# The indexer's query-key products with both parts of a query head stacked in the array's 128 rows

## The chip, the cores and the metric

One core of a Trainium2 chip runs the program in one launch. The metric is the device time of that launch in microseconds. Below, PE is TensorE, DVE is VectorE, ACT is ScalarE, POOL is GpSimd and SP is SyncE, which issues most of the transfers.

## What is computed

One layer of a decoder block on 512 tokens of width 1024, all in fp32:

```
h = rms_norm(x);  proj = h @ w_in            # columns for all mixers and gates
# A: sparse attention; the indexer picks 128 causal keys for each query
dots  = einsum('bqhd,bsd->bqhs', iq, ik)     # 8 index heads of 64, one key head
score = einsum('bqh,bqhs->bqs', iw, relu(dots))
sel   = top_k(causal(score), 128)
y_att = softmax attention of 8 heads over the selected keys
# B: chunked gated DeltaNet, 4 heads of 128, after a short convolution
# merge
x = x + (sigmoid(ga) * (y_att @ w_att) + sigmoid(gb) * (y_dn @ w_dn)) @ w_o
# PEER: 8 product-key heads, top 16 each, over 128 * 128 experts
x = x + peer(rms_norm(x))
```

## The kernel before, in words

Activations lie transposed: features on the 128 partitions, the 512 tokens along the free axis. Most products are made in a split format: an fp32 operand is written as a high part of type fp32r, which ACT copies, and a low part, which DVE gets by subtraction (`split`), and three fp32r products stand for one fp32 product (`mm3`).

**First stage (to about 464 us of the profile).** `project(ct)` makes 128 of the projection's columns: it loads a weight tile `wt` of 512 KB, splits it into `wh` and `wl`, and does 24 products. The tiles `wt`, `wh` and `wl` come from the pool `pp`, two buffers each. 43 such projections follow each other: one small one with the index keys, 12 convolved ones for the DeltaNet, 4 index queries (`CT_IQ`), 4 for the output gate z, k, v, 4 attention queries, and 16 merge gates, which are stored to DRAM (`sgd`). From the sixth on they are the filler of four chains that run step by step in turn: two DeltaNet pairs, the indexer and the attention. After each step of a chain, a fraction `FILL_A` or `FILL_B` of a projection's step is added, and `tc.issue_after` ties it to a product of that chain. A scheduler then sets the order on each engine from its own estimate of times.

**The indexer.** `projections()` copies the four results of 128 rows (two heads each) to `iqT`; the index keys are copied to rows 0 to 63 of `ikT`, and a transfer repeats them in rows 64 to 127. `index(tb)`, for blocks 1 to 3 of 128 queries, makes for each of the 8 heads one plain fp32 product of 64 rows:

```
            b = (h % 2) * 64
            dt = bank("at")
            mm(dt[:, :N], iqT[b:b + 64, h // 2, dsl], ikT[b:b + 64, :N])
```

N is 256, 384 or 512 keys. ACT takes the positive part, DVE adds it with its weight, and 16 rounds on DVE pick the top 128.

**Branches and output (464 to 561 us).** `attention_branch` makes 8 tiles (dt) of the attention branch: a gate is loaded back from `sgd` and passed through a sigmoid, half a weight tile of 256 KB goes through `wt`, `wh` and `wl`, 12 products follow. The DeltaNet branch does the same 8 times (L701 to L710 for the gate, the reading of the products and the sum, then a split of the sum into `mh` and `ml`). The output product takes 8 weight tiles of 512 KB, four for each half `cg` of the columns; block b of four has its bank `acc[b]`. In the second half, the weights of kp 0 and 1 go to tiles of their own (`late`), and block 3 is tied behind the transposes of block 0, which follow `second_norm(0)`. All of these weights pass through `wt` in `pp`, and so do the first two of the PEER query (`wq`).

**PEER (561 us to the end).** Its weights come from other pools (`wp`, `up`, `ex`): 128 tiles of u, a top-k, 128 tiles of v, and gathered rows for the last block of tokens.

Of the kernel before, what the change touches and what calls it, by code (L numbers as in the profile page):

```python
# [9 lines left out]
F32 = mybir.dt.float32  # L10
F32R = mybir.dt.float32r
# [4 lines left out]
ALU = mybir.AluOpType  # L16
# [3 lines left out]
P = 128  # L20
T = 512
D = 1024
NB = T // P
# [5 lines left out]
CT_DN, CT_SM, CT_IQ, CT_K, CT_V, CT_Q, CT_Z, CT_G = 0, 12, 13, 17, 18, 19, 23, 27  # L29
# [53 lines left out]
def tile_block(ctx, tc, x, xT, w_in, sc_cols, sc_rows, w_br, w_o, w_q, subT, uT, uv, cst, iota, out, dbg=None):  # L83
    nc = tc.nc
    dbg = dbg or {}
    V, S, G, PE = nc.vector, nc.scalar, nc.gpsimd, nc.tensor
# [3 lines left out]
    def mm(o, l, r, start=True, stop=True):  # L90
        hop[0] = PE.matmul(o, l, r, start=start, stop=stop).ins  # L91
# [9 lines left out]
    def load(dst, src):  # L101
        nc.sync.dma_start(dst, src)
# [5 lines left out]
    def pool(stack, name, **kw):  # L108
        return stack.enter_context(tc.tile_pool(name=name, bufs=1, **kw))
# [13 lines left out]
    hl = hp.tile([P, 8, T], F32R, name="hl", tag="hl")  # L123
    fm = pool(f1, "fm")
    pp = pool(px, "pp", side="right")
# [5 lines left out]
    def bank(tag, bufs=2):  # L131
        return ps.tile([P, T], F32, name=tag, tag=tag, bufs=bufs)

    def tmp(n=T, bufs=5):
        return pp.tile([P, n], F32, name="tmp", tag=f"tmp{n}", bufs=bufs)
# [30 lines left out]
    def split(hi, lo, src):  # L166
        S.copy(hi, src)  # L167
        return V.tensor_tensor(lo, src, hi.bitcast(F32), op=ALU.subtract).ins  # L168
# [16 lines left out]
    rb = bank("dn0")  # L185
    for tb in range(NB):
        mm(hs(rb, tb), r1[:, tb:tb + 1].to_broadcast([P, P]), ident)
    rbs = pp.tile([P, T], F32, name="rbs")
    S.copy(rbs, rb)
    lows = []  # L190
    for k in range(8):
# [3 lines left out]
        lows.append(split(hh[:, k, :], hl[:, k, :], xk))  # L195

    def weights(wp, src, shape=(8, P), dst=None):
        wt = wp.tile([P, *shape], F32, name="wt", bufs=2)
        load(wt, src)
        wh, wl = dst or (wp.tile([P, *shape], F32R, name=n, bufs=2) for n in ("wh", "wl"))  # L200
        split(wh, wl, wt)
        return wh, wl

    def project(ct):

        wh, wl = weights(pp, w_in[ct])
        o = bank("mm")
        for k in range(8):
            mm3(o, (wh[:, k, :], wl[:, k, :]), (hh[:, k, :], hl[:, k, :]), k == 0, k == 7)
            if k < 7:  # L210
                yield
        return o

    ikT = fm.tile([P, T], F32, name="ikT")
    iqT = fm.tile([P, 4, T], F32, name="iqT")
    kT = fm.tile([P, T], F32, name="kT")
    vtok = fm.tile([P, NB, P], F32, name="vtok")
    small = fm.tile([P, NB, 16], F32, name="small")
# [23 lines left out]
    both, early, o = project(CT_SM), conv(0), None  # L242
    while o is None:
        try:
            next(both)
        except StopIteration as e:
            o = e.value
        next(early)
    sm_ = tmp()
    S.copy(sm_, o)  # L250
    S.copy(ikT[0:64, :], o[0:64, :])
    nc.sync.dma_start(ikT[64:128, :], ikT[0:64, :])
    st = bank("at")
    for tb in range(NB):
        PE.transpose(st[:, tb * P:(tb + 1) * P], sm_[:, tb * P:(tb + 1) * P], ident)
    V.tensor_copy(small, st.rearrange("p (b c) -> p b c", c=P)[:, :, 64:80])
    t3 = [P, NB, 4]
    u = pp.tile(t3, F32, name="u")
    e = pp.tile(t3, F32, name="e")
    al = pp.tile([P, 4], F32, name="al")  # L260
    V.tensor_tensor(u, small[:, :, 8:12], dtb[:, None, :].to_broadcast(t3), op=ALU.add)
    V.scalar_tensor_tensor(e, u, -1.0, u, op0=ALU.mult, op1=ALU.min)
# [190 lines left out]

    def projections():
        for t in range(4):
            S.copy(iqT[:, t, :], (yield from project(CT_IQ + t)))
            if t == 3:
                done.add("index")
            yield
        for t in range(4):  # L460
            S.activation(szT[:, t, :], (yield from project(CT_Z + t)), AF.Silu)
            if t == 3:
                done.add("z")
            yield
        o = yield from project(CT_K)
        kk = tmp()
        S.activation(kk, o, AF.Square)
        kss = bank("at")
        mm(kss, blk64, kk)
        S.activation(kT, o, AF.Copy, scale=kg)  # L470
        V.tensor_scalar(kk, kss, 1.0 / 64, EPS, op0=ALU.mult, op1=ALU.add)
        rk = tmp()
        rsqrt(rk, kk, "k")
        V.tensor_tensor(kT, kT, rk, op=ALU.mult)
        yield
        o = yield from project(CT_V)
        va = tmp()
        S.copy(va, o)
        vt = bank("at")
        for tb in range(NB):  # L480
            PE.transpose(hs(vt, tb), hs(va, tb), ident)
        S.copy(vtok.rearrange("p b c -> p (b c)"), vt)
        yield
        for j in range(4):
            o = yield from project(CT_Q + j)
            S.activation(qT[:, j, :], o, AF.Copy, scale=qg)
            q2 = tmp()
            S.activation(q2, o, AF.Square)
            qs = bank("at")
            for tb in range(NB):  # L490
                mm(qs[:, tb * 2:tb * 2 + 2], hs(q2, tb), ind2)
            V.tensor_scalar(qsc[:, :, 2 * j:2 * j + 2], qs[:, :8].rearrange("p (b c) -> p b c", c=2), 1.0 / 64, EPS, op0=ALU.mult, op1=ALU.add)
            if j < 3:
                yield
        q_ = pp.tile([P, NB * 8], F32, name="q_")
        fl = qsc.rearrange("p b h -> p (b h)")
        rsqrt(q_, fl, "q")
        V.tensor_scalar(fl, q_, 0.125, None, op0=ALU.mult)
        done.add("attention")
        yield  # L500
        for t in (8 * br + dt for dt in range(8) for br in range(2)):
            o = yield from project(CT_G + t)
            s_ = tmp()
            S.copy(s_, o)
            nc.sync.dma_start(sgd[t], s_)
            yield
# [6 lines left out]
    def index(tb):  # L513
        N = (tb + 1) * P
        dsl = slice(tb * P, (tb + 1) * P)
        acc = row("acc", 1)
        for h in range(8):
            b = (h % 2) * 64
            dt = bank("at")
            mm(dt[:, :N], iqT[b:b + 64, h // 2, dsl], ikT[b:b + 64, :N])  # L520
            yield
            R = row("R", 2)
            S.activation(R[:, :N], dt[:, :N], AF.Relu)
            w = small[:, tb, h:h + 1]
            if h == 0:
                V.tensor_scalar(acc[:, :N], R[:, :N], w, 0.0, op0=ALU.mult, op1=ALU.add)
            else:
                V.scalar_tensor_tensor(acc[:, :N], R[:, :N], w, acc[:, :N], op0=ALU.mult, op1=ALU.add)
        V.tensor_tensor(acc[:, dsl], acc[:, dsl], cs("causneg"), op=ALU.add)
        wk = row("wk", 1)  # L530
        for r in range(16):
            m8 = aw.tile([P, 8], F32, name="m8", bufs=2)
            src = acc if r == 0 else wk
            V.max(m8, src[:, :N])
            V.match_replace(wk[:, :N], m8, src[:, :N], TAKEN)
        bias = row(f"bias{tb}", 1)
        V.scalar_tensor_tensor(bias[:, :N], wk[:, :N], 0.0, acc[:, :N], op0=ALU.add, op1=ALU.is_equal)
        V.tensor_scalar(bias[:, :N], bias[:, :N], -1e30, None, op0=ALU.mult)
        return bias
# [75 lines left out]
    def attention_branch():  # L615

        ya = hp.tile([P, 2, 4, T], F32R, name="ya", tag="hh")
        mixed = branch[0] = hp.tile([P, 8, T], F32, name="mixed", tag="hl")
        for k in range(4):
            split(ya[:, 0, k], ya[:, 1, k], qT[:, k, :])  # L620
        for dt in range(8):
            s_ = tmp()
            load(s_, sgd[dt])
            S.activation(s_, s_, AF.Sigmoid)
            wt = pp.tile([P, 8, P], F32, name="wt", bufs=2)[:, :4]
            load(wt, w_br[dt][:, :4])
            w = [pp.tile([P, 8, P], F32R, name=n, bufs=2)[:, :4] for n in ("wh", "wl")]
            split(*w, wt)
            o = bank("mm")
            for k in range(4):  # L630
                mm3(o, at(w, k), (ya[:, 0, k], ya[:, 1, k]), k == 0, k == 3)
                if k < 3:
                    yield
            V.tensor_tensor(mixed[:, dt, :], s_, o, op=ALU.mult)
            yield
# [62 lines left out]
    for dt in range(8):  # L698
        s_ = tmp()
        load(s_, sgd[8 + dt])  # L700
        S.activation(s_, s_, AF.Sigmoid)  # L701
        wt = pp.tile([P, 8, P], F32, name="wt", bufs=2)[:, :4]
        load(wt, w_br[dt][:, 4:])
        w = [pp.tile([P, 8, P], F32R, name=n, bufs=2)[:, :4] for n in ("wh", "wl")]
        split(*w, wt)
        o = bank("mm")
        for k in range(4):
            mm3(o, at(w, k), at(yd, k), k == 0, k == 3)
        V.tensor_tensor(s_, s_, o, op=ALU.mult)
        V.tensor_tensor(s_, s_, branch[0][:, dt, :], op=ALU.add)  # L710
        split(mt[0][:, dt, :], mt[1][:, dt, :], s_)
# [83 lines left out]
    wp = pool(wx, "wp", side="right", reuse_waits="tile")  # L795
# [41 lines left out]
    for h in range(8):  # L837
# [3 lines left out]
        for p in range(2):  # L841
            if h == 0:
                _, o = first_q[p]
            else:
                o = bank("mm")
# [159 lines left out]
    n, slot = 0, 0  # L1005
# [135 lines left out]
```

## Time and profile before

| | |
|---|---|
| median of 3 runs | 1843.3 us (1842.14 to 1844.12) |
| profiled execution, its own time | 1844.26 us |
| its span, first to last instruction | 1842.5 us |
| PE busy | 1791.8 us, 97% |
| DVE busy | 1442.0 us, 78% |
| ACT busy | 803.1 us, 44% |
| POOL busy | 188.6 us, 10% |
| mean granted clock of PE | 0.998 of full speed |

Times in the trace count from the span's start. A row of the timeline gives start, duration, engine, line and operation, the tile written and the tiles read, and in brackets how long the engine was idle before it and what ended that. Products on PE are pipelined: the distance of two starts is what one costs, and a row's own duration is longer. A plain fp32 product appears as two passes.

### The profile page before, as it was taken

What the parts mean: (1) busy time and instruction counts of PE and PEld (TensorE: products, weight loads), DVE (VectorE), ACT (ScalarE), POOL (GpSimd) and SP (SyncE); (2) the same over time, 40 slices, a digit from 0 to 9 for tenths busy, and PEclk for the clock granted to TensorE, in tenths of its full rate; (3) what the DMA queues carried; (4) which work ended last, traced back from release to release, by engine and by line L of the source; (5) the groups of instructions that cost most, each with busy time, mean ns of one, the idle gap of its engine ahead of it and who ended that gap; (6) DMA issues with size and microseconds to landing.
All of it is one profiled execution on the core that took longest, in us unless ns stands there. A gap on an engine that the chain in (4) does not pass through costs nothing.

```text
span 1842.5 us, 26292 instructions
## 1 busy us (share of the span) xinstructions
PE 1791.8 (97%) x9527; PEld 1572.5 (85%) x9527; DVE 1442.0 (78%) x3291; ACT 803.1 (44%) x1401; POOL 188.6 (10%) x132
## 2 busy tenths in 40 slices
PE   5999999999999999999999999999999999999998
PEld 4787677878788899999999988888888888888887
DVE  5767988654667899999997686788787887787886
ACT  5433434443533334555655444344443444343442
POOL 0000000000000000010000112122121222212220
PEclk9999999999999999999999999999999999999999
DMA  4211111111643214567676898989988988898974
GB/s 148 92 64 63 58 41 58 52 52 41 211 147 130 89 52 142 186 226 258 250 268 228 307 365 305 336 316 361 337 313 327 347 315 309 335 357 313 343 299 170
DMA packets 142354, 396.74 MB, mean 215 GB/s; under 512 B 10704, under 2 KB 71760, under 8 KB 122768
## 3 DMA queue, kind: packets, MB, share of 16 engines
q1 hardware_dynamic: 123792, 260.84, 40.3%
q0 software_dynamic: 18432, 134.23, 18.9%
q8 instruction: 75, 1.23, 0.3%
q14 instruction: 55, 0.45, 0.1%
HBM read 353.60 MB, written 41.29 MB: 214 GB/s over the span
## 4 chain that ended last, share of the span: by engine, by line
PE 82%; DVE 8%; DMA 6%; ACT 2%; issue 1%; SPq 0%; DVEq 0%; ACTq 0%
PE mm L91 28%; PE acc L91 25%; PE wo L91 6%; PE dn L91 5%; PE at L91 3%; DMA vt<-in_uv_dram 2%; DMA gt<-gd 2%; DVE ul L168 1%; DVE ob L986 1%; PE tr L91 1%; PE at L571 0%; PE dn L320 0%; DMA wt<-in_w_br_dram 0%; DVE tmp L229 0%; DVE gt L1046 0%
## 5 line engine op out<-in xcount | busy, mean ns | idle before, releaser
L91 PE MATMUL acc<-vl,ch 128*128 128x512 f32 x768 | 299.5, 390 | 1.1 <-DVE vl L1045 1.1
L91 PE MATMUL acc<-vh,cl 128*128 128x512 f32 x768 | 298.2, 389 | 0.0
L91 PE MATMUL acc<-vh,ch 128*128 128x512 f32 x768 | 263.1, 390 | 4.9 <-ACT vh L1044 4.9
L951 POOL DMA_INDIRECT row<-in_uv_dram,eidx x124 | 178.6, 1441 | 832.3 <-DVE x1g L963 775.1
L167 ACT CAST uh<-ut 128x1024 fp32r<-128x1024 f32 x128 | 134.6, 1051 | 150.0 <-PE mm L91 84.0
L1045 DVE TENSOR_TENSOR vl<-vt,vh 128x1024 fp32r<-128x1024 f32 x128 | 156.4, 1222 | 50.3 <-ACT vh L1044 47.6
L168 DVE TENSOR_TENSOR ul<-ut,uh 128x1024 fp32r<-128x1024 f32 x128 | 155.9, 1219 | 34.4 <-ACT uh L167 33.8
L91 PE MATMUL mm<-hTh,uh 128*128 128x384 f32 x496 | 168.6, 340 | 2.9 <-ACT gs L818 1.9
L91 PEld LDWEIGHTS acc<-vh,ch 128*128 128x128 f32 x768 | 143.3, 188 | 32.1 <-ACT vh L1044 6.6
L91 PE MATMUL mm<-hTh,ul 128*128 128x384 f32 x496 | 168.0, 340 | 2.7 <-DVE ul L168 2.7
L91 PEld LDWEIGHTS acc<-vl,ch 128*128 128x128 f32 x768 | 144.2, 188 | 30.2 <-DVE vl L1045 2.1
L963 DVE SCALAR_TENSOR_TENSOR x1g<-row,co,x1g 128x1024 f32<-128x1024 f32 x128 | 163.8, 1280 | 7.4 <-ACT co L962 5.3
L91 PEld LDWEIGHTS acc<-vh,cl 128*128 128x128 f32 x768 | 144.1, 188 | 29.2
L1044 ACT CAST vh<-vt 128x1024 fp32r<-128x1024 f32 x128 | 133.9, 1046 | 78.4 <-DMA vt<-in_uv_dram 64.0
L91 PE MATMUL mm<-hTl,uh 128*128 128x384 f32 x496 | 167.3, 337 | 0.0
L167 ACT CAST ch<-gt 128x384 fp32r<-128x384 f32 x128 | 65.5, 512 | 218.1 <-PE acc L91 211.1
L960 DVE CUSTOM_DVE_ANT_0 scr<-row,h2g 128x1024 f32<-128x1024 f32 x128 | 156.0, 1218 | 0.3
L91 PE MATMUL mm<-hh,wh 128*128 128x512 f32 x344 | 144.6, 424 | 3.6 <-ACT hh L167 2.1
L168 DVE TENSOR_TENSOR wl<-wt,wh 128x1024 fp32r<-128x1024 f32 (+1 forms) x81 | 90.1, 1115 | 63.4 <-ACT wh L167 63.2
L91 PE MATMUL mm<-hh,wl 128*128 128x512 f32 x344 | 137.3, 401 | 0.0
L91 PE MATMUL mm<-hl,wh 128*128 128x512 f32 x344 | 136.9, 398 | 0.0
L167 ACT CAST wh<-wt 128x1024 fp32r<-128x1024 f32 (+1 forms) x81 | 77.7, 962 | 110.9 <-PE mm L91 86.7
(818 smaller groups left out, 3765.8 us busy)
## 6 DMA issues: line engine op xcount, KB each, us to landing
ut<-in_uT_dram SPq DMA_DIRECT2D x128, 512.0 KB
vt<-in_uv_dram SPq DMA_DIRECT2D x128, 512.0 KB
gd<-gb SPq DMA_DIRECT2D x24, 1024.0 KB
gt<-gd SPq DMA_DIRECT2D x16, 1536.0 KB
wt<-in_w_in_dram SPq DMA_DIRECT2D x43, 512.0 KB
gs<-gs SPq DMA_DIRECT2D x84, 192.0 KB
wt<-in_w_q_dram SPq DMA_DIRECT2D x16, 512.0 KB
sgd<-tmp SPq DMA_DIRECT2D x16, 256.0 KB
```

The costliest lines, as they stand in the source:

```text
L91: hop[0] = PE.matmul(o, l, r, start=start, stop=stop).ins
L167: S.copy(hi, src)
L168: return V.tensor_tensor(lo, src, hi.bitcast(F32), op=ALU.subtract).ins
L951: G.indirect_dma_start(out=row.rearrange("p t d -> p (t d)"), out_offset=None, in_=uv, in_offset=bass.IndirectOffsetOnAxis(ap=released.get ...
L960: V.tensor_tensor_reduce(scr, row[:, 0], h2g, 1.0, 0.0, op0=ALU.mult, op1=ALU.add, accum_out=a)
L963: V.scalar_tensor_tensor(x1g, row[:, 1], co, x1g, op0=ALU.mult, op1=ALU.add)
L986: V.tensor_scalar(ob[:, t], io, sl[:, 1, n:n + 1], sl[:, 2, n:n + 1], op0=ALU.is_equal, op1=ALU.mult)
L1044: S.copy(vh, vt)
L1045: paced = V.tensor_tensor(vl, vt, vh.bitcast(F32), op=ALU.subtract)
```

## The change

The index operands are kept in split form, and a head's product takes all 128 rows. For each head, `iqS[:, h]` holds the high part in its own half of the rows and the low part in the other half. `ikS` holds the keys' high part in both halves, and in a second tile their low part in both halves. Two fp32r products of 128 rows, accumulated in one bank, then give all four partial products.

```
-    ikT = fm.tile([P, T], F32, name="ikT")
-    iqT = fm.tile([P, 4, T], F32, name="iqT")
+    ikS = [fm.tile([P, T], F32R, name=f"ik{n}") for n in "hl"]
+    iqS = fm.tile([P, 8, T], F32R, name="iqS")
...
-    S.copy(ikT[0:64, :], o[0:64, :])
-    nc.sync.dma_start(ikT[64:128, :], ikT[0:64, :])
+    S.copy(ikS[0][0:64, :], o[0:64, :])
+    V.tensor_tensor(ikS[1][0:64, :], o[0:64, :], ikS[0][0:64, :].bitcast(F32), op=ALU.subtract)
+    for part in ikS:
+        load(part[64:128, :].bitcast(F32), part[0:64, :].bitcast(F32))
...
-            S.copy(iqT[:, t, :], (yield from project(CT_IQ + t)))
+            o = yield from project(CT_IQ + t)
+            hi, lo = tmp().bitcast(F32R), tmp().bitcast(F32R)
+            split(hi, lo, o)
+            for i in range(2):
+                mine, other = slice(i * 64, i * 64 + 64), slice(64 - i * 64, 128 - i * 64)
+                load(iqS[mine, 2 * t + i, :].bitcast(F32), hi[mine].bitcast(F32))
+                load(iqS[other, 2 * t + i, :].bitcast(F32), lo[mine].bitcast(F32))
...
-            b = (h % 2) * 64
             dt = bank("at")
-            mm(dt[:, :N], iqT[b:b + 64, h // 2, dsl], ikT[b:b + 64, :N])
+            for i, part in enumerate(ikS):
+                mm(dt[:, :N], iqS[:, h, dsl], part[:, :N], i == 0, i == 1)
```

The larger tiles need room. The change takes it from `wt` in `pp`, which now has one buffer, in `weights` and in both branches, and from four small tiles (`rbs`, `u`, `e`, `q_`), which now come from the rotating `tmp`:

```
-        wt = wp.tile([P, *shape], F32, name="wt", bufs=2)
+        wt = wp.tile([P, *shape], F32, name="wt", bufs=1 if wp is pp else 2)
...
-            wt = pp.tile([P, 8, P], F32, name="wt", bufs=2)[:, :4]
+            wt = pp.tile([P, 8, P], F32, name="wt", bufs=1)[:, :4]
```

The order moves in three places that matter here. On SP, where the last gates are stored (`sgd`) and the first branch weights are loaded from `in_w_br_dram`, before:

```order
L505 DMA sgd6_296<-tmp_3799 128x512
L102 DMA wt_4192<-in_w_br_dram 128x512
L505 DMA sgd14_304<-tmp_3929 128x512
L102 DMA wt_4215<-in_w_br_dram 128x512
L505 DMA sgd7_297<-tmp_4065 128x512
L102 DMA tmp_4189<-sgd0_290 128x512
L102 DMA tmp_4212<-sgd1_291 128x512
L505 DMA sgd15_305<-tmp_4176 128x512
```

and now:

```order
L514 DMA sgd15_308<-tmp_4231 128x512
L102 DMA tmp_4267<-sgd1_294 128x512
L102 DMA wt_4270<-in_w_br_dram 128x512
L102 DMA tmp_4290<-sgd2_295 128x512
L102 DMA tmp_4313<-sgd3_296 128x512
L102 DMA tmp_4336<-sgd4_297 128x512
L102 DMA x1g_4441<-in_x_dram 128x1024
L102 DMA wt_4293<-in_w_br_dram 128x512
```

The second branch weight (`wt_4215`, now `wt_4270`) moved from ahead of the last two gate stores to behind them.

On DVE in the DeltaNet branch (the reading of the products at L709, now L718; the sum at L710, now L719; the weight's low part `wl` and the sum's low part `ml` at L168), before:

```order
L168 TENSOR_TENSOR wl_4522<-wt_4519,wh_4521 128x512
L709 TENSOR_TENSOR tmp_4490<-tmp_4490,mm_4499 128x512
L168 TENSOR_TENSOR ml_4411<-tmp_4464,mh_4410 128x512
L168 TENSOR_TENSOR wl_4548<-wt_4545,wh_4547 128x512
L710 TENSOR_TENSOR tmp_4490<-tmp_4490,mixed_4180 128x512
```

and now:

```order
L718 TENSOR_TENSOR tmp_4493<-tmp_4493,mm_4502 128x512
L168 TENSOR_TENSOR wl_4525<-wt_4522,wh_4524 128x512
L719 TENSOR_TENSOR tmp_4493<-tmp_4493,mixed_4235 128x512
L168 TENSOR_TENSOR ml_4466<-tmp_4493,mh_4465 128x512
L718 TENSOR_TENSOR tmp_4519<-tmp_4519,mm_4528 128x512
L168 TENSOR_TENSOR wl_4551<-wt_4548,wh_4550 128x512
```

Before, `wl_4522` is the weight of the step after `mm_4499` and stands ahead of the reading of `mm_4499`; now `wl_4525`, the weight of the step after `mm_4502`, stands behind the reading of `mm_4502`.

On PE at the end of the output product's second half (`wo_4748` to `wo_4751` are blocks 0 to 3, now `wo_4803` to `wo_4806`; `tr` are the transposes of block 0's norm `h2t`), before:

```order
L91 MATMUL wo_4750<-wh_4770,mh_4410 128x512
L91 MATMUL wo_4750<-wl_4771,mh_4410 128x512
L91 MATMUL wo_4750<-wh_4770,ml_4411 128x512
L728 MATMUL tr_4844<-C_92,h2t_4827 128x128 x4
L728 MATMUL tr_4851<-C_92,h2t_4827 128x128 x4
L91 MATMUL wo_4751<-wh_4752,mh_4410 128x512
```

and now:

```order
L91 MATMUL wo_4803<-wh_4825,ml_4466 128x512
L91 MATMUL wo_4804<-wl_4826,mh_4465 128x512
L91 MATMUL wo_4804<-wh_4825,ml_4466 128x512
L91 MATMUL wo_4804<-wh_4825,mh_4465 128x512
L91 MATMUL wo_4804<-wl_4826,mh_4465 128x512
L91 MATMUL wo_4804<-wh_4825,ml_4466 128x512
L91 MATMUL wo_4805<-wl_4826,mh_4465 128x512
L91 MATMUL wo_4805<-wh_4825,ml_4466 128x512
L91 MATMUL wo_4805<-wh_4825,mh_4465 128x512
L91 MATMUL wo_4805<-wl_4826,mh_4465 128x512
L91 MATMUL wo_4805<-wh_4825,ml_4466 128x512
L737 MATMUL tr_4899<-C_92,h2t_4882 128x128 x4
```

Before, blocks 0 and 1 are finished ahead of the 24 products of block 2, and block 0's transposes follow those; now blocks 0, 1 and 2 take the last weight (`wh_4825`, `wl_4826`) one after the other, 5 products each, right ahead of block 0's transposes.

## Rows read from the trace of the kernel before

**Rows 1.** Windows: length, busy us (PE, PEld, DVE, ACT, POOL), PEclk, DMA share, GB/s
```profile
100.00:464.00 364.00, 357.77 (x2022) 282.00 (x2020) 251.68 (x747) 142.94 (x307) 0.00 (x0) 1.00 0.15 53
...
600.00:1842.50 1242.50, 1224.79 (x6539) 1118.12 (x6538) 1036.76 (x2202) 549.32 (x928) 188.42 (x128) 1.00 0.76 276
```

**Rows 2.** Waits of PE from 100 to 464 us: us in total, times, longest (first, last of 4)
```profile
PE dn L91 <- ACT s L385: 3.3, 6, 0.7
...
PE mm L91 <- ACT tmp L504: 0.5, 1, 0.5
```

**Rows 3.** Timeline of PE, index passes of three widths: start us, us, what, xcount
```profile
150.00 0.70 PE L91 MATMUL at<-ikT,iqT 64*128 64x256 f32 x2
150.63 0.50 PE L91 MATMUL mm<-hh,wh 128*128 128x512 f32 x1
...
161.79 0.70 PE L91 MATMUL at<-ikT,iqT 64*128 64x256 f32 x4
...
169.90 0.91 PE L91 MATMUL at<-ikT,iqT 64*128 64x384 f32 x2
...
218.53 1.12 PE L91 MATMUL at<-ikT,iqT 64*128 64x512 f32 x2
```

**Rows 4.** Timeline of PE, split-type products of 512 and of 384 columns
```profile
260.63 0.39 PE L91 MATMUL mm<-hl,wh 128*128 128x512 f32 x1
260.86 0.39 PE L91 MATMUL mm<-hh,wl 128*128 128x512 f32 x1
...
566.68 0.34 PE L91 MATMUL mm<-hTl,wq 128*128 128x384 f32 x1
...
567.21 0.34 PE L91 MATMUL mm<-hTl,wq 128*128 128x384 f32 x1
```

**Rows 5.** Tile wt up to 460 us: ns min/median/max, first and last start us, forms
```profile
L167 ACT CAST wh<-wt x43: 1028/1046/1054, 14.3 to 449.1; 128x1024 fp32r<-128x1024 f32 x43
L168 DVE TENSOR_TENSOR wl<-wt,wh x43: 1206/1225/1228, 15.5 to 450.2; 128x1024 fp32r<-128x1024 f32 x43
```

**Rows 6.** Tile wt from 460 to 620 us, same columns
```profile
L167 ACT CAST wh<-wt x31: 600/623/1056, 462.1 to 615.2; 128x512 fp32r<-128x512 f32 x16, 128x1024 fp32r<-128x1024 f32 x15
L168 DVE TENSOR_TENSOR wl<-wt,wh x31: 678/693/1227, 462.8 to 616.4; 128x512 fp32r<-128x512 f32 x16, 128x1024 fp32r<-128x1024 f32 x15
```

**Rows 7.** Timeline of SP's queue and of ACT: two loads and their readers
```profile
504.73 0.33 SPq L102 DMA_DIRECT2D tmp<-sgd  x1
...
507.34 0.63 ACT L701 ACTIVATE tmp<-tmp 128x512 f32<-128x512 f32 x1 [0.77 <-DMA tmp<-sgd]
...
539.37 3.30 SPq L102 DMA_DIRECT2D wt<-in_w_q_dram  x2
...
542.97 1.05 ACT L167 CAST wq<-wt 128x1024 fp32r<-128x1024 f32 x1 [1.90 <-DMA wt<-in_w_q_dram]
```

**Rows 8.** Timeline of ACT, DVE and PE in the branch and output stages
```profile
469.80 0.39 ACT L416 ACTIVATE s<-dn 128x256 f32<-128x256 f32 x1
...
506.13 0.69 DVE L709 TENSOR_TENSOR tmp<-tmp,mm 128x512 f32<-128x512 f32 x1 [0.23 <-PE mm L91]
...
514.29 0.69 DVE L709 TENSOR_TENSOR tmp<-tmp,mm 128x512 f32<-128x512 f32 x1 [0.22 <-PE mm L91]
...
548.03 0.68 DVE L754 TENSOR_TENSOR x<-x,wo 128x512 f32<-128x512 f32 x1
...
552.92 1.28 DVE L723 SCALAR_TENSOR_TENSOR h2t<-x,r,rowv 128x1024 f32<-128x1024 f32 x1
...
561.02 0.39 PE L91 MATMUL wo<-wh,ml 128*128 128x512 f32 x1
```

**Rows 9.** Windows with PE alone: length, PE busy, PEclk, DMA share, GB/s
```profile
494.50:495.00 0.50, 0.00 (x0) 1.00 1.08 365
...
496.50:497.00 0.50, 0.50 (x2) 0.50 0.32 123
...
582.00:583.00 1.00, 1.00 (x5) 0.50 0.79 324
```

More of the change, by code (lines that the diff above doesn't have):

```diff
@@ L187, in tile_block @@
         mm(hs(rb, tb), r1[:, tb:tb + 1].to_broadcast([P, P]), ident)
-    rbs = pp.tile([P, T], F32, name="rbs")
+    rbs = tmp()
     S.copy(rbs, rb)
@@ L257, in tile_block @@
     t3 = [P, NB, 4]
-    u = pp.tile(t3, F32, name="u")
-    e = pp.tile(t3, F32, name="e")
+    u, e = (tmp()[:, :NB * 4].rearrange("p (b h) -> p b h", h=4) for _ in range(2))
     al = pp.tile([P, 4], F32, name="al")
@@ L494, in projections @@
                 yield
-        q_ = pp.tile([P, NB * 8], F32, name="q_")
+        q_ = tmp()[:, :NB * 8]
         fl = qsc.rearrange("p b h -> p (b h)")
@@ L701, in tile_block @@
         S.activation(s_, s_, AF.Sigmoid)
-        wt = pp.tile([P, 8, P], F32, name="wt", bufs=2)[:, :4]
+        wt = pp.tile([P, 8, P], F32, name="wt", bufs=1)[:, :4]
         load(wt, w_br[dt][:, 4:])
```

## The prediction

> **What bounds the kernel now.** I read first the busy times of two long stretches. From 100 to 464 us TensorE (PE) is busy 357.8 of 364 us, VectorE (DVE) 251.7 and ScalarE (ACT) 142.9; from 600 us to the end PE is busy 1224.8 of 1242.5 [rows 1]. A busy PE could still be a waiting one, so I read its waits next: four kinds in 364 us, 6.2 us in all, 3.3 us the longest kind [rows 2]. So in the first stretch a microsecond taken from PE is a microsecond won as long as its inputs keep coming, and in the second whatever happened before is carried to the end one to one. Third, what the index products cost; fourth, how a weight tile travels (load, ACT's copy to the high part, DVE's subtraction for the low part), because the change pays for its larger index tiles with the second `wt` buffer, in every user of `wt` in that pool.
>
> **1. The index products: -7.6 us.** The 24 heads of the three index blocks stand on PE as 48 passes of 64 rows (two a head), in 19 events. A lone head of 256 columns holds PE from 150.00 to 150.63, 0.07 less than its row's 0.70; of 384 columns 0.91, so 0.84; of 512 columns 1.12, so 1.05 [rows 3]. Events: 5 of 256, 7 of 384, 7 of 512 columns: 5 x 0.63 + 7 x 0.84 + 7 x 1.05 = 16.4 us. There are fewer events than heads because two heads that stand next to each other lie in different halves of the rows and take the time of one: four passes at 161.79 in 0.70, like two at 150.00 [rows 3]. This happens 5 times.
>
> The new form is 48 products of 128 rows in the split type. Such products follow each other at 0.23 us with 512 columns (260.63 to 260.86) and at 0.177 with 384 (three in 0.53 us from 566.68 to 567.21) [rows 4]. 256 columns are not in the trace: between half of the 512 (0.12) and the 384 (0.177), I take 0.14. Sum 16 x (0.23 + 0.177 + 0.14) = 8.8 us, between 8.4 and 9.3. Gain 16.4 - 8.8 = 7.6 us, 7.1 to 8.0.
>
> A rule speaks against this part. The Trainium skill (TensorE: Matmul & The Clock Gate, Part 3: Packing small matmuls — row/col tiling) says that products which use few rows run at the same time when they lie in different row groups, so that the old form was not wasteful in itself. The trace agrees where two heads meet [rows 3], but only 10 of 24 heads do; were all 12 pairs packed, the old form would cost 4 x (0.63 + 0.84 + 1.05) = 10.1 us and the gain would be 1.3, not 7.6.
>
> **2. What the new operands cost: +1 us.** Four subtractions for the queries and one for the keys on DVE (0.69 us each, from the subtraction of a 512-wide tile [rows 6]) are 3.4 us on an engine with 112 us idle in that stretch [rows 1]: nothing; if that cover were gone, 3.4. ACT's copies keep their number. SP issues 17 more transfers, and the index waits for them. In the new order the first two index heads stand behind another 24 projection products (24 x 0.23 = 5.6 us), while copy, subtraction and a transfer behind a weight load (0.6 + 0.7 + 3.6 [rows 6, 7]) take about 5 to 7 us: 0 to 3, I take 1.
>
> **3. One `wt` buffer, projections: +2 us.** With one buffer a load is issued only when the subtraction of the weights before has ended. Load to copy takes 3.6 us for 512 KB (issued 539.37, ACT starts 542.97 after waiting for it) [rows 7], the copy 1.05, the subtraction 1.23 [rows 5]: a ring of 5.9 us. The 43 copies lie on average (449.1 - 14.3)/42 = 10.4 us apart [rows 5], so the ring fits, save where projections follow back to back at 24 x 0.23 = 5.6 us. That is so for some ten of them: 0 to 6, I take 2.
>
> **4. One `wt` buffer, branch and output products: +32 us.** Here the work between two weights is shorter than the ring, and this decides the case. A 256 KB load takes 2.6 us to its reader (504.73 to 507.34) [rows 7]; I take 2.7, since a stored gate is loaded beside it. With 0.62 for the copy and 0.69 for the subtraction [rows 6] a branch step cannot be shorter than 4.0 us. Before, the second branch ran at (514.29 - 506.13)/3 = 2.72 us a step [rows 8], twelve products. The new order on DVE gives the same 4.0 by another way: each subtraction stands behind the reading of the step before (0.69 + 0.69, then ten products at 0.23, and the pipe).
>
> Chain, step by step. Before, both first branch weights were loaded ahead. Now the load for dt 1 stands in SP's queue behind the last gate store, and ACT reaches its copy after the pair-1 copy at 469.80 [rows 8]: 470.2, subtraction done 471.5. Then 14 branch steps, 14 x 4.0 = 56; one step stands behind 1.5 MB of x and four subtractions for `yl`: +1.2; then 8 output weights, 8 x 5.9 = 47. The last subtraction ends at 471.5 + 56 + 1.2 + 47 = 575.7. Five products later block 0 is complete (576.9). From there its norm took 548.03 to 554.20 before, 6.2 us [rows 8]; now block 1's small operations (12 x 0.19) and a subtraction of `wq` (1.23) are interleaved: 9.7, so 586.6. In the new order block 3 stands behind block 0's transposes, with nothing left to do for PE meanwhile: 0.9 + 24 x 0.23 = 6.5, so 593.1. Before, the last output product ended at 561.4 [rows 8]. Difference +31.7, say 32. Were a load only 2.2 and 3.1 us, the chain would be 14 x 0.5 + 8 x 0.5 = 11 shorter: +21. Were the branch steps 4.5, it would be +39.
>
> **5. The clock: +1.5 us.** After PE's idle time at 494 to 496 the granted clock is half (1.2 GHz) at 496.5 [rows 9]. Two new gaps (some 2 us ahead of the output products, 8 ahead of block 0's transposes) would each cost one such stretch: 0 to 3.
>
> **Sum.** The profiled execution took 1844.26 us for a span of 1842.5. 1844.3 - 7.6 + 1 + 2 + 32 + 1.5 = 1873; the median of the runs is 1 us below the profiled execution: **1872 us**. After block 3 both orders are the same and PE is the bound [rows 1], so nothing is won back.
>
> **Rivals.**
> *The single buffer is hidden; faster.* If a load, copy and subtraction fit in the products of one step, part 4 vanishes and part 1 remains: 1843 - 7.6 + 1 to 3, about 1838 us. It decides at a ring of 2.8 us in the branches and 5.6 in the output products. For it: the projections show that loads are mostly early enough. Against: the rows give 4.0 and 5.9. Chance 0.10. In between, with loads at their shortest and PE's order filling the gaps, 1846 to 1860: 0.14.
> *The clock falls in the branches; slower still.* PE would idle 1.3 us in each 4.0. Half clock doubles the ten products behind each subtraction, +2 a step: 28 us for 14 steps, and some half of that if it comes and goes, about 1886. For it: half clock after the 2 us gap at 494, and at 582 just after a gap of about 1 us between small products [rows 9]. Against: the gaps here stand between products of full width, twelve to a step. Chance 0.18.
> *The change does not pay where it says.* If the new products ran no faster than the old pairs, part 1 falls to 1 and the time is 1879: 0.05, inside the range.
> *A draw*, part 4 eaten to about a third: 0.04.
>
> **How the numbers follow.** Forecast (1860 to 1882) 0.49, 0.05 for no gain from the products, 0.18 colder, 0.14 in between, 0.10 faster, 0.04 a draw. The range 1850 to 1893 leaves out the faster case, the draw and the edge of the two neighbours, 2 in 10. A measurement of this kernel can tell about 0.2%, 3.7 us, from no change. Faster 0.10, same 0.04, slower 0.86.
>
> **What would show it.** Right: index rows of 128 rows at 0.14 to 0.24 us each, no wait of PE above 3 us before 464; `wh` copies in the branches waiting for DMA in nearly every step, 4 us apart; the last output product some 27 us later than before; the stretch from there to the end as long as before. Wrong: branch steps still near 2.8 us, or PE waiting for `iqS`, or projections stretched by more than 6 us before 464.

## The result, and the profile after

The changed kernel takes 1877.99 us in the median of 6 runs (1871.21 to 1886.28), the kernel before 1842.77 us (1841.51 to 1857.24, 6 runs): a ratio of 1.0168, 95% interval 1.0141 to 1.0195. The profiled execution of after took 1877.3 us, its span 1875.5 us, 33.0 more than before's 1842.5. The page of after gives for its engines:

```profile
PE 1800.0 (96%) x9527; PEld 1578.7 (84%) x9527; DVE 1445.0 (77%) x3296; ACT 803.2 (43%) x1401; POOL 190.1 (10%) x132
```

PE is busy 8.2 us longer than before (1791.8), so most of the 33 us are time in which it stands still.

Where the 33.0 us lie is read from the first and last start of PE's products, tile by tile: `hh` is the input of the projections, `yh` that of the DeltaNet branch, `mh` that of the output products, `hTh` that of PEER. The rows give count, shortest/median/longest ns, first and last start. Before:

```profile
L91 PE MATMUL mm<-hh,wh x344: 388/397/794, 19.8 to 462.6; 128*128 128x512 f32 x172
...
L91 PE MATMUL mm<-yh,wl x32: 388/389/628, 491.6 to 516.6; 128*128 128x512 f32 x32
...
L91 PE MATMUL wo<-wh,mh x64: 387/389/475, 516.8 to 560.6; 128*128 128x512 f32 x64
...
L91 PE MATMUL mm<-hTh,wh x112: 389/389/662, 584.4 to 672.6; 128*128 128x512 f32 x112
```

And after:

```profile
L91 PE MATMUL mm<-hh,wh x344: 389/397/795, 20.1 to 457.3; 128*128 128x512 f32 x172
...
L91 PE MATMUL mm<-yh,wl x32: 388/397/628, 497.9 to 531.4; 128*128 128x512 f32 x32
...
L91 PE MATMUL wo<-wh,mh x64: 387/389/775, 534.0 to 594.2; 128*128 128x512 f32 x64
...
L91 PE MATMUL mm<-hTh,wh x112: 389/389/499, 618.8 to 706.7; 128*128 128x512 f32 x112
```

| stretch, ended by the last (first) start of | before | after | difference |
|---|---|---|---|
| projections and index, last `hh` | 462.6 | 457.3 | -5.3 |
| branches, last `yh` | 54.0 | 74.1 | +20.1 |
| output products, last `wo` | 44.0 | 62.8 | +18.8 |
| first queries, first `hTh,wh` | 23.8 | 24.6 | +0.8 |
| from there to the span's end | 1258.1 | 1256.7 | -1.4 |

So the part that the change is about wins 5.3 us, and the two stages behind it lose 39. The last stretch, PEER, has the same work in every run; in the profiled executions of all runs together it takes 1256 to 1269 us, so its -1.4 says nothing. What PE waits for from 457 to 600 us says how the 39 are lost (total us, times, longest):

```profile
PE mm L91 <- ACT wh L167: 12.7, 12, 2.5
PE wo L91 <- ACT wh L167: 5.5, 5, 2.2
PE tr L737 <- DVE rs_a L162: 5.0, 1, 5.0
```

Twelve times the branch products wait for the copy of their weight, five times the output products do, and block 0's transposes stand still for 5.0 us behind its norm (`rs_a` is a tile of the norm). Before, the same stretch has two waits for a `wh`, together 2.2 us:

```profile
PE mm L91 <- ACT wh L167: 2.2, 2, 2.0
```

ACT's copies themselves wait for the loads (start us, us, engine, operation, in brackets its idle time and what ended it):

```profile
484.32 0.62 ACT L167 CAST wh<-wt 128x512 fp32r<-128x512 f32 x1 [3.11 <-DMA wt<-in_w_br_dram]
...
505.86 0.62 ACT L167 CAST wh<-wt 128x512 fp32r<-128x512 f32 x1 [1.40 <-DMA wt<-in_w_br_dram]
```

and the next load waits for the subtraction on DVE, here with the row of the transfer on SP's queue:

```profile
507.15 0.69 DVE L718 TENSOR_TENSOR tmp<-tmp,mm 128x512 f32<-128x512 f32 x1 [1.97 <-PE mm L91]
507.76 0.68 DVE L168 TENSOR_TENSOR wl<-wt,wh 128x512 fp32r<-128x512 f32 x1
...
508.47 0.33 SPq L102 DMA_DIRECT2D wt<-in_w_br_dram  x1
```

The copy of 505.86 ends at 506.5, but its subtraction starts only at 507.76, behind the reading of the step before (L718), and the load for the next step leaves at 508.47, when that subtraction has ended: the ring of load, copy and subtraction can be followed in four rows.

The new index products, by contrast, are nearly as cheap as hoped. Rows of heads of 256, 384 and 512 columns (compare [rows 3]):

```profile
128.52 0.28 PE L91 MATMUL at<-ikh,iqS 128*128 128x256 f32 x1
128.63 0.28 PE L91 MATMUL at<-ikl,iqS 128*128 128x256 f32 x1
...
203.04 0.35 PE L91 MATMUL at<-ikh,iqS 128*128 128x384 f32 x1
203.22 0.34 PE L91 MATMUL at<-ikl,iqS 128*128 128x384 f32 x1
...
213.94 0.40 PE L91 MATMUL at<-ikl,iqS 128*128 128x512 f32 x1
214.18 0.39 PE L91 MATMUL at<-ikh,iqS 128*128 128x512 f32 x1
```

Their distances are 0.11, 0.18 and 0.24 us. Where the first product of a head follows other work, it takes longer: some 0.26 us with 384 columns and 0.32 with 512 (210.09 to 210.41). Counted from each start to the next, all 48 products cost some 9.2 us against 16.4 before.

### The profile page after: what moved, and what is told of

The parts are those of the page before. It is cut to its first block, busy times and chain, and to the rows that moved or that the text cites. A ratio compares the mean times of both kernels' runs of the same rounds, so it can differ in the third digit from the quotient of the medians.

```text
span 1875.5 us, 26330 instructions
## 1 busy us (share of the span) xinstructions
PE 1800.0 (96%) x9527; PEld 1578.7 (84%) x9527; DVE 1445.0 (77%) x3296; ACT 803.2 (43%) x1401; POOL 190.1 (10%) x132
## 3 DMA queue, kind: packets, MB, share of 16 engines
q0 software_dynamic: 18432, 134.23, 18.6%
## 4 chain that ended last, share of the span: by engine, by line
PE 75%; DVE 11%; DMA 8%; ACT 3%; issue 2%; SPq 0%; DVEq 0%; ACTq 0%
PE acc L91 25%; PE mm L91 24%; PE dn L91 5%; PE wo L91 4%; PE at L91 3%; DVE ul L168 2%; DMA gt<-gd 2%; DMA wt<-in_w_o_dram 2%; DVE wl L168 1%; DMA vt<-in_uv_dram 1%; DMA wt<-in_w_br_dram 1%; ACT wh L167 1%; DMA wt<-in_w_in_dram 1%; PE tr L91 1%; DVE ob L995 1%
## 5 line engine op out<-in xcount | busy, mean ns | idle before, releaser
L168 DVE TENSOR_TENSOR ul<-ut,uh 128x1024 fp32r<-128x1024 f32 x128 | 155.7, 1218 | 36.4 <-ACT uh L167 36.1
L168 DVE TENSOR_TENSOR wl<-wt,wh 128x1024 fp32r<-128x1024 f32 (+1 forms) x81 | 90.4, 1116 | 89.9 <-ACT wh L167 87.8
```

## The experiments

All ratios are to the kernel before on the same chip, with their 95% intervals. The scheduler sets the order on the engines anew for each run, so a run with another number of buffers shows what the buffers cost together with the order that comes with them; no run changes the order of the late stages alone.

**1. The kernel before with one `wt` buffer** (the second edit in both branches)**.**

```
-        wt = wp.tile([P, *shape], F32, name="wt", bufs=2)
+        wt = wp.tile([P, *shape], F32, name="wt", bufs=1 if wp is pp else 2)
...
-            wt = pp.tile([P, 8, P], F32, name="wt", bufs=2)[:, :4]
+            wt = pp.tile([P, 8, P], F32, name="wt", bufs=1)[:, :4]
```

> The kernel before with one change: the weight tile wt in pp has one buffer, everywhere. Theory (the single buffer costs the whole loss, the index products give some 7 us back): slower than the changed kernel by about 7 us, so 1880 to 1892 us, with branch steps of 4.0 to 4.4 us and output weights 5.9 us apart. Rival (the new operands, with their transfers and the order that follows from them, cause part of the loss): below 1875 us. Rival (the buffer was hidden): within 4 us of 1843.

Measured: 1892.52 us, ratio 1.0239 (1.0214 to 1.0263), half a microsecond above the range of its theory. The buffer alone costs more than the whole change (1.0168), so no part of the loss has to be put on the new operands. The distance to the changed kernel is some 13 us, not 7. The trace shows where the rest arises: the last `hh` product starts at 470.7 us, 8.1 later than before. The rows from 20 us to there, first of the kernel before, then of this run, give length, busy us of PE, PEld, DVE, ACT and POOL, granted clock, DMA share, GB/s:

```profile
20.00:462.60 442.60, 432.15 (x2345) 341.58 (x2346) 304.16 (x840) 184.15 (x364) 0.00 (x0) 1.00 0.17 58
...
20.00:470.70 450.70, 438.92 (x2346) 344.90 (x2347) 306.42 (x841) 185.32 (x364) 0.00 (x0) 0.98 0.17 58
```

With the same products PE is busy 6.8 us longer and stands still only 1.3 us longer; its waits for `wh` and `wl` there are two, of 0.6 and 0.5 us. The granted clock is half in three pieces of the first stage (234 to 238, 244 to 248 and 306 to 313 us), 13.7 us in all, which the kernel before has not; work of 6.8 us that takes 13.7 is just the longer busy time. It is no accident of one execution: over the whole span the mean granted clock of run 1's five executions is 0.989 to 0.992, that of the 23 of the kernel before beside them 0.994 to 0.999. So the direct waits for the single buffer are about 1 us here, and the rest goes with the clock; why the clock fell in this order was not tried.

**2. The changed kernel with two buffers again.** `iqS` holds all 512 queries, but the index products read blocks 1 to 3 alone. With 384 of them it leaves 4 KB per partition, the size of a `wt`:

```
...
-    iqS = fm.tile([P, 8, T], F32R, name="iqS")
+    iqS = fm.tile([P, 8, T - P], F32R, name="iqS")
...
-                load(iqS[mine, 2 * t + i, :].bitcast(F32), hi[mine].bitcast(F32))
...
+                load(iqS[mine, 2 * t + i, :].bitcast(F32), hi[mine, P:].bitcast(F32))
...
-                mm(dt[:, :N], iqS[:, h, dsl], part[:, :N], i == 0, i == 1)
+                mm(dt[:, :N], iqS[:, h, (tb - 1) * P:tb * P], part[:, :N], i == 0, i == 1)
...
```

> The changed kernel, with wt in pp back at two buffers; the room comes from iqS, which keeps only the 384 queries that the index products read (blocks 1 to 3). Theory: 1843 less 7 to 8 for the products, plus about 1 for their operands: 1834 to 1839 us, and nearly the whole loss of 35 us gone. Rival (the new operands themselves cost): 1843 or more. Rival (the new order of the branch and output stages is what costs, whatever the buffers): above 1850.

Measured: 1837.61 us, 0.9955 (0.9932 to 0.9978), and in a second series, on another chip,

> The version with two wt buffers and 384 queries once more, beside the two others on one chip: 0.3 to 0.7 per cent faster than the kernel before, 1831 to 1840 us.

1839.18 us, 0.9968 (0.9951 to 0.9986). The loss is gone, and the kernel is faster than before by 4 to 8 us. The tile rows of the first series show the branches at 508.9 - 458.0 = 50.9 us (54.0 before) and the output products at 44.0, as before; block 0's transposes wait for nothing again:

```profile
L91 PE MATMUL mm<-hh,wh x344: 388/397/794, 20.2 to 458.0; 128*128 128x512 f32 x172
...
L91 PE MATMUL mm<-yh,wl x32: 388/389/499, 487.0 to 508.9; 128*128 128x512 f32 x32
...
L91 PE MATMUL wo<-wh,mh x64: 389/389/476, 509.1 to 552.9; 128*128 128x512 f32 x64
...
L91 PE MATMUL mm<-hTh,wh x112: 389/389/502, 578.6 to 666.5; 128*128 128x512 f32 x112
```

**3 and 4. One buffer in the projections only, and everywhere but there.** A counter names the tile, `wt` or `wtb` with one buffer each, and is advanced for the stages that are to have two:

```
+    def wt_name(stage):
+        turns[0] += {"proj": 0, "br": 1, "wo": 1}[stage]
+        return ("wt", "wtb")[turns[0] % 2]
```

(`0, 1, 1` in the first, `1, 0, 0` in the second; both with the 384 queries.)

> As the run with two buffers, but the projections use one buffer alone and the branches, the output products and the first weights of wq take turns with a second tile. Theory (the projections' ring of 5.9 us is hidden but for some 2 us): 1836 to 1842, at most 6 above the run with two buffers. Rival (the loss is made in the projections too): over 1848.

> The opposite: two tiles in turn for the projections, one for the branches, the output products and wq. Theory: the whole loss stays but for the projections' 0 to 6 us, 1870 to 1882 us. Rival (the loss is made in the projections): under 1850.

Measured: 1842.46 us, 0.9985 (0.9965 to 1.0005), half a microsecond above its theory, and 1877.42 us, 1.0176 (1.0149 to 1.0202). The loss is made in the branches and the output products. What one buffer costs in the projections, these two do not settle to better than some 5 us. Run 3 is slower than run 2 by 4.9 us in the medians, and by 5.7 with an interval of 4.8 to either side in the means. But run 4, with two tiles in the projections, is no faster than the changed kernel with one (1.0176 and 1.0168). In the traces no cost can be seen there: the last `hh` starts at 456.8 with one buffer and at 458.0 with two, and PE's waits from 20 to 457 us name no `wh` or `wl`, neither in run 3 nor in the changed kernel.

**5. Two tiles of half the size.** The same 4 KB as in the changed kernel, cut in two (a branch weight takes one of them):

```
-        wt = wp.tile([P, *shape], F32, name="wt", bufs=1 if wp is pp else 2)
-        load(wt, src)
...
-        split(wh, wl, wt)
+        parts = 2 if wp is pp else 1
+        n = shape[0] // parts
+        for i in range(parts):
+            wt = wp.tile([P, n, shape[1]], F32, name="wt", bufs=2)
+            load(wt, src[:, i * n:(i + 1) * n])
+            split(wh[:, i * n:(i + 1) * n], wl[:, i * n:(i + 1) * n], wt)
...
```

> The changed kernel with its 4 KB of wt per partition cut in two tiles of 2 KB: every weight of 512 KB is loaded, copied and subtracted in two halves, a branch weight (256 KB) is one half. No byte more than in the changed kernel, but two loads can be under way. Theory (it is the one load at a time that costs, not the missing bytes): a half takes 2.7 + 0.62 + 0.69 = 4.0 us with two of them under way, so 2.0 a branch step (2.7 of products) and 4.0 an output weight (5.6 of products): hidden, 1836 to 1844 us. Rival (the bytes, or the many more instructions on ACT and DVE, decide): 1860 or more.

Measured: 1854.35 us, 1.0038 (1.0014 to 1.0061): between the two theories. The tile rows and PE's waits tell which part was right:

```profile
L91 PE MATMUL mm<-yh,wl x32: 389/389/497, 492.3 to 513.7; 128*128 128x512 f32 x32
...
L91 PE MATMUL wo<-wh,mh x64: 389/389/775, 514.0 to 565.1; 128*128 128x512 f32 x64
```

```profile
PE tr L740 <- DVE rs_a L162: 5.0, 1, 5.0
PE tr L740 <- DVE hTl L743: 1.0, 1, 1.0
```

The branches take 513.7 - 460.1 = 53.6 us (the last `hh` starts at 460.1), as in the kernel before (54.0): there the ring of load, copy and subtraction is hidden. The output products take 51.4 instead of 44.0. The two waits shown are PE's longest from 457 to 580 us, and no wait for an output weight of 0.5 us or more is left; but the 5.0 us ahead of block 0's transposes are still there. Block 0's norm has no products left beside it in this order, and the granted clock is half from 555 to 562 us, around the end of that wait. So of the 18.8 us of the output stage some 7 go with the order of its second half; this is read from the trace, as no run changes that order alone.

**6 and 7. One buffer in the branches alone, and in the output products alone** (`1, 0, 1` and `1, 1, 0`).

> Two tiles in turn for projections, output products and wq, one for the branches alone. Theory (the parts of the loss add): the branches' 16 steps cost 20 us more, the rest nothing, 1852 to 1862 us. Rival (one waits behind the other, so that a late branch hides the output weights' loads): the branches alone give over 25 us, above 1864.

> Two tiles in turn for projections and branches, one for the output products and wq. Theory: output weights 5.9 us apart instead of 5.6 and block 0's norm left uncovered at the end, 16 to 20 us, so 1852 to 1860 us. Rival (the output products' loss comes only from the late branches, as 5.9 is hardly more than 5.6): under 1846.

Measured: 1862.1 us, 1.0086 (1.0054 to 1.0117), at the upper end of its theory, and 1856.21 us, 1.0059 (1.0037 to 1.008), within its own. Against run 2's 0.9955 these are 1.31 and 1.04%, 24 and 19 us. Together that is 43 us, and both at once (run 4) gave 1.0176 - 0.9955 = 2.21%, 41 us. The traces say it stage by stage, here the last rows of run 6, then of run 7:

```profile
L91 PE MATMUL mm<-yh,wl x32: 388/391/502, 500.7 to 534.5; 128*128 128x512 f32 x32
L91 PE MATMUL wo<-wh,mh x64: 389/389/497, 531.4 to 579.0; 128*128 128x512 f32 x64
...
L91 PE MATMUL mm<-yh,wl x32: 388/389/499, 487.5 to 510.7; 128*128 128x512 f32 x32
L91 PE MATMUL wo<-wh,mh x64: 388/390/776, 512.5 to 572.6; 128*128 128x512 f32 x64
```

From the last `hh` (459.9 and 459.0) the branches take 74.6 us in run 6 and 51.7 in run 7, the output products 44.5 and 61.9; run 2 has 50.9 and 44.0, run 4 73.1 and 63.5. Each stage loses alone what it loses beside the other: the two losses add up, and neither hides behind the other.

**8. The old form with its heads in pairs.** In the kernel before, the two heads of a pair are issued together into two banks:

```
+        for pr in range(4):
+            two = [bank("at") for _ in range(2)]
+            for i, dt in enumerate(two):
+                b = i * 64
+                mm(dt[:, :N], iqT[b:b + 64, pr, dsl], ikT[b:b + 64, :N])
...
```

> The kernel before with the two heads of a pair issued together into two banks, in the old form and with two wt buffers, so that the 64-row passes of both halves can lie side by side. Theory (two heads in different halves take the time of one): each pair that stands together on PE shows four passes in the time of two, and where all 12 did, 16.4 us would become 10.1; 8 of 12 stand together here, so 2 to 3 us less on PE and 1839 to 1846 us in all. Rival (pairs don't overlap): no change of the index passes on PE.

Measured: 1843.74 us, 0.9985 (0.9963 to 1.0007), no difference that can be told, though within its theory. The passes do lie side by side where the scheduler leaves them together, but it does not always:

```profile
149.86 0.70 PE L91 MATMUL at<-ikT,iqT 64*128 64x256 f32 x4
...
194.77 0.91 PE L91 MATMUL at<-ikT,iqT 64*128 64x384 f32 x2
...
245.42 1.54 PE L91 MATMUL at<-ikT,iqT 64*128 64x512 f32 x4
```

All four pairs of 256 columns stand as four passes in 0.70 us. Of the wider ones some are apart, and one pair overlaps only in part (1.54 us where two heads one after the other would take 2.1); 7 of the 12 pairs overlap whole. The last `hh` product starts at 460.7, 1.9 us earlier than before.

**9 and 10. Other places for the projections.** Two settings of the fillers in the kernel of run 2: `FILL_A = 0.9, LAG = 10` and `FILL_A = 0.7, LAG = 10`.

> The version with two wt buffers and 384 queries, with FILL_A 0.9 in place of 0.85 and LAG 10 in place of 6: other places for the projections between the steps of the DeltaNet. In the version with 0.85 and 6 PE makes 11 us of small DeltaNet products with no projection between them at 222 to 234 us, waits 4 us there, and the granted clock is half for 7 us. Theory (the shorter index products left that stretch bare, and the bare stretch costs its waits and the clock): with the longest bare piece at 30 products instead of 35 and its place changed, 0 to 4 us faster than the same kernel with 0.85 and 6. Rival (another order opens other gaps): the same or slower, and half clock elsewhere in the first stage.

> As the run before with FILL_A 0.7 and LAG 10: longest bare piece 29 products, the next ones 27 and 26. Theory: no stretch of half clock between 100 and 457 us, the projections end 3 to 5 us earlier, 2 to 5 us faster than with 0.85 and 6. Rival: fewer projections in the first part move the gaps to the end of the first stage, the same or slower.

Measured: 1836.89 us, 0.9965 (0.9945 to 0.9984), and 1847.92 us, 1.0019 (1.0001 to 1.0037), beside run 2's second series at 1839.18 us, 0.9968. The first can't be told from that; it lies in the range of its theory (0 to 4 us faster) and of its rival alike. The second is some 9 us slower, and its theory has fallen: the last `hh` starts at 472.2 us, 16.3 later than in the second series of run 2. From 20 us until then PE stands still for 20.8 us instead of 11.8. Of the 200 us from 100 to 300 it is busy 183.9, there 192.9: the gaps lie there and not at the end of the stage, where its rival put them. The granted clock is half at 230 to 241 us in the first and at 39 to 42 and 277 to 285 us in the second, for 10 us in each, and 6.8 us in the second series of run 2. What a better order would be worth stays open.

## Why the prediction was right

The forecast was 1872 us (1850 to 1893), slower with a chance of 0.86. Measured 1878, within the range. Against the measured span difference of 33.0 us the sum had 28.9. That it came so near is in part luck: part 4 was 7.7 us short, and part 5, whose cost lies in the same stages, the first stage and the last stretch made up for 3.6 of it.

- **Part 1, index products -7.6:** 16.4 became some 9.2, so -7.2 [rows 3, 4], at the low end of its 7.1 to 8.0. The rule of the Trainium skill (TensorE: Matmul & The Clock Gate, Part 3: Packing small matmuls — row/col tiling) is borne out by run 8, four passes in the 0.70 us of two: two heads in different halves take the time of one. But the pairs have to stand together, and here the order on PE decided how many did. Run 8 won nothing that can be told from the time.
- **Parts 2 and 3, +3:** they, with the products, gave -4.6 at the end of the first stage, and -5.3 was measured. The terms inside were not as foretold. PE waits for no `iqS`, and 0.8 us for the low part of the keys. The one buffer brought no wait in the projections. PE stands still for 13.0 us from 20 us to the last `hh`, 10.5 before, and half clock, which I had put elsewhere, came in two pieces (below).
- **Part 4, +32:** the mechanism, the two places and the order of the steps were right, the size was too small. Branches, output products and first queries lost 20.1 + 18.8 + 0.8 = 39.7 us, near the +39 that I had named for a branch step of 4.5. The chain from the second branch weight's copy to the last output weight's subtraction was put at 575.7 - 470.2 = 105.5 us. It ran from 465.07 to 577.29, so 112.2:

```profile
465.07 0.62 ACT L167 CAST wh<-wt 128x512 fp32r<-128x512 f32 x1 [0.21 <-DMA wt<-in_w_br_dram]
...
527.84 0.62 ACT L167 CAST wh<-wt 128x512 fp32r<-128x512 f32 x1 [1.48 <-DMA wt<-in_w_br_dram]
...
538.71 1.05 ACT L167 CAST wh<-wt 128x1024 fp32r<-128x1024 f32 x1 [4.21 <-DMA wt<-in_w_o_dram]
...
575.00 1.04 ACT L167 CAST wh<-wt 128x1024 fp32r<-128x1024 f32 x1 [4.74 <-DMA wt<-in_w_o_dram]
576.07 1.22 DVE L168 TENSOR_TENSOR wl<-wt,wh 128x1024 fp32r<-128x1024 f32 x1 [4.56 <-ACT wh L167]
```

- **The mis-sized term is the branch step, 4.0 us.** From the copy at 465.07 to that at 527.84 lie 14 steps, 62.8 us, 4.48 each, where 14 x 4.0 + 1.2 = 57.2 was forecast: 5.6 of the 6.7 us. I took 2.7 us for the load from one row [rows 7]. From the end of a subtraction to the next copy it was 2.64 to 4.48 us, 3.05 in the mean (for 4 of the 14 copies the profile names PE or DVE, not the load, as what came last). Eight of the 14 are at most 2.83, so the row was a usual one; what it could not show is the spread: the longest followed the 1.5 MB of x, for which the sum had 1.2 us, the next a gate load. Copy and subtraction, 1.34, were as assumed, but for the one step shown above, where the order on DVE added 1.25.
- **Output weights, 5.9 a step:** from 538.71 to 575.0 their copies lie 6.05 us apart, one of 7.0 among them. From the last subtraction to the end of the last output product it took 18.6 us (to 595.9), where 17.4 was forecast. Block 0's norm was quicker, 7.4 us instead of 9.7, and what follows it slower, 9.9 instead of 6.5; that these nearly cancel is luck. The last output product ended 34.5 us later than before, not some 27.
- **Part 5, the clock +1.5:** of the two places that I had named, one came. Ahead of the output products PE stood still for 2.2 us, and the granted clock stayed 1.00. Behind the 5.0 us ahead of block 0's transposes it was half until about 591 us: the eight transposes took 1.6 us instead of 0.8, and the next nine products of block 3 3.8 us instead of 2.1. That is 2.5 us, and PE had nothing else to do beside them. The columns are those of run 1's rows:

```profile
485.50:488.50 3.00, 3.00 (x8) 2.20 (x8) 0.17 (x1) 0.80 (x3) 0.00 (x0) 0.50 0.27 87
...
503.00:505.00 2.00, 2.00 (x6) 1.48 (x6) 1.32 (x3) 0.62 (x1) 0.00 (x0) 0.50 0.31 103
...
586.00:591.00 5.00, 4.92 (x16) 4.28 (x17) 3.83 (x6) 3.06 (x5) 0.00 (x0) 0.50 0.03 11
...
230.00:236.00 6.00, 5.28 (x23) 4.47 (x22) 6.00 (x20) 0.76 (x2) 0.00 (x0) 0.50 0.00 0
```

In the branches two pieces of some 3.5 us followed the waits of 2.5 and 2.0 us. The ring set the pace there, so the step from 484.32 to 488.36 was 4.0 us all the same. Two more pieces, 48.5 to 52 and 229.5 to 236.5, lie in the first stage, which had none before.
- **The rivals:** a hidden buffer is refuted by runs 1, 4, 6 and 7. Half clock at every branch step did not come: two pieces in 16 steps. Products no faster than the old is refuted by the rows.

## What to carry to other kernels

A buffer that pays for a new tile is priced in every stage that rotates through it, not in the stage that is changed: the sum of load, copy and release there against the work of one step (here 4.5 against 2.7 us in the branches) tells the loss, and that PE was busy for 97% of the time before does not protect against it. Before a buffer is given up, look for room in the new tile itself: a quarter of `iqS` was never read, and leaving it out turned a loss of 1.7% into a gain of 0.3 to 0.45%. For a load on a ring, take the mean of many loads of that stage, with what stands ahead of them in the queue, and not a single row: here the row gave 2.6 us and was a usual one, while the loads went up to 4.48.

## What was not expected of the hardware

- In the first stage the clock fell in the profiled execution of every run, of the old form too (runs 1 and 8), for the longer pieces mostly among DeltaNet products that wait for one another, and not in that of before, whose other executions have mean granted clocks from 0.991 to 0.999. Two executions of the same program (runs 2 and 11) had 10.2 and 6.8 us of half clock before 470 us, and their last `hh` products started at 458.0 and 455.9. So a gain of a few us can be spent after gaps of about a microsecond or less: the waits ahead of the piece at 229.5 us in after are 0.4 to 1.1 us long, and PE is busy for 4.3 of the 7 us from 222 to 229.
- From the first `hTh,wh` product to the end, the profiled executions of runs 1 to 11 took 1256 to 1269 us, those of runs 2 and 11, the same program, 1262.6 and 1268.7. That spread is as large as the gain in question, so the gain needed its two series of 12 runs; and no single profiled time decides here.
